# RWKV-7 chunk products moved from half-array tiles to the two diagonal quarters of the array

## The chip, the cores and the metric

One core of a Trainium2 chip runs the whole layer in one launch. The metric is the device time in microseconds, median over runs. Five engines work side by side, each through its own instruction queue in order: TensorE (PE; its weight loads are shown apart as PEld), VectorE (DVE), ScalarE (ACT), GpSimd (POOL) and SyncE (SP, which issues the transfers).

## The reference

A decoder layer on 2048 tokens with model width 1024: an mLSTM group and an RWKV-7 group side by side, then cross-attention into 256 memory tokens, then a SwiGLU block, all in float32. The change touches the RWKV-7 group alone: 8 heads of width 64, each with a 64x64 state that is updated token by token, and a layer norm over each head's 64 outputs:

```python
def rwkv7_scan(r, w, k, v, a, b):
    def step(S, inp):
        r_t, w_t, k_t, v_t, a_t, b_t = inp
        sa = jnp.einsum('bhij,bhj->bhi', S, a_t)
        S = S * w_t[:, :, None, :] + sa[..., None] * b_t[:, :, None, :] + v_t[..., None] * k_t[:, :, None, :]
        return S, jnp.einsum('bhij,bhj->bhi', S, r_t)
...
    y = rwkv7_scan(r, hs(decay), k, v, -kk, kk * a)
    mean = jnp.mean(y, -1, keepdims=True)
    var = jnp.mean(jnp.square(y - mean), -1, keepdims=True)
    y = (y - mean) * lax.rsqrt(var + RWKV_LN_EPS)
```

## The kernel before

The program has a first pass over the input, then the *mixer* (both groups), then the output projection, attention and the SwiGLU block. The mixer makes four passes (`hp` 0 to 3), one per pair of RWKV heads and one mLSTM head. The two RWKV heads of a pair lie in partitions 0 to 63 and 64 to 127. A pass goes over 8 segments of 256 tokens, each cut into 4 chunks of 64 tokens. A *unit* below is one segment of one pass; there are 32.

For each unit, `prepare` projects k, r and v (tiles `kps`, `rps`, `vps`, three half-precision products for each of 8 blocks of the width), computes decays and gates, and builds the chunk matrices: `AR` (decayed a and r), `KB` (decayed k and b), their products with the causal mask (`aps`, line 379), the transposed `KB` (`kbps`, line 391) and the transposed v (line 368). `solve` then inverts the triangular matrices of two units at a time on GpSimd, with small 32x32 products (`pps`, `xps`). `scan` carries the state over the chunks. Its chain for one chunk is: product `ch` column 0 (line 458), copy to `R` on ScalarE (460), product column 1 with `M` (467), copy to `VX` (470), product column 2 (472), and the state update on VectorE (476), which the next chunk's first product waits for. The outputs of four chunks are made at the end of the unit (`yps`, lines 482 and 485), normalised in `tail` and transposed back (`tps`, line 504). `mlstm` does the other group, with its own projections (`qps`, `vops`).

Before, the scan keeps two terms on top of each other in 128 partitions: `VS[:, n, h]` holds the state of head h in that head's 64 partitions and the values v in the other 64, `RR`, `KBt` and `VX` are laid out to match. So one product with 128 rows and 64 columns adds state term and value term in one go. The two heads' products write to the two column halves of the array.

The order of the instructions on each engine is set when the program is built, by a scheduler that follows its own estimates of the times and the dependencies; the code's order is only a start. Buffers come from pools; `pax` has two banks of PSUM for all small results of `prepare`.

Of the kernel before, what the change touches and what calls it, by code (L numbers as in the profile page):

```python
# [105 lines left out]
def rwkv_consts(c, pool, I):  # L106
    nc = c.nc
    par = c.par
    c.mu_s = pool.tile([P, 14], F32, name="mu_s")
    nc.vector.tensor_scalar(c.mu_s, par[:, R_MU:R_MU + 14], DSC, None, op0=ALU.mult)  # L110
    c.mu_c = pool.tile([P, 14], F32, name="mu_c")
    nc.vector.tensor_scalar(c.mu_c, par[:, R_MU:R_MU + 14], -DSC, DSC, op0=ALU.mult, op1=ALU.add)
    c.bones = pool.tile([P, P], F32, name="bones")
    nc.vector.memset(c.bones, 0.0)
    nc.vector.memset(c.bones[0:64, 0:64], 1.0)
    nc.vector.memset(c.bones[64:128, 64:128], 1.0)
    c.ind = pool.tile([P, 2], F32, name="ind")
    nc.vector.memset(c.ind, 0.0)
    nc.vector.memset(c.ind[0:64, 0:1], 1.0)
    nc.vector.memset(c.ind[64:128, 1:2], 1.0)  # L120
# [124 lines left out]
def mixer_pass(c, I, hp, tp, T):  # L245
# [48 lines left out]

    def prepare(sg, u, M):
        g = Ctx()
# [5 lines left out]
        AR = tp.t1.tile([P, 4, P], F32, tag="AR", name="AR")  # L302
        g.RR = next(tp.RR)
        g.M = M
        g.AY = sl.tile([P, 4, 2, 64], F32, tag="AY", name="AY")
        g.KBt = sl.tile([P, 4, 2, 64], F32, tag="KBt", name="KBt")
        g.VS = sl.tile([P, 4, 2, 64], F32, tag="VS", name="VS")
        g.VX = sl.tile([P, 4, 2, 64], F32, tag="VX", name="VX")
        g.bon = sl.tile([P, SGN], F32, tag="bon", name="bon")
        g.W = sl.tile([P, 4, 1], F32, tag="W", name="W")  # L310
        KB = tp.t1.tile([P, 4, 192], F32, tag="KB", name="KB")
# [48 lines left out]
        nc.scalar.copy(KB[:, :, 128:192], KB[:, :, 0:64])  # L360
# [5 lines left out]
        vps = tp.pax.tile([P, 2, P], F32, tag="ax", name="vps")  # L366
        for m in range(2):
            nc.tensor.transpose(vps[:, m], v[:, m * P:(m + 1) * P], c.ident)
        for h in range(2):
            for e in range(2):  # L370
                nc.scalar.copy(g.VS[halves[1 - h], e::2, h], vps[halves[e], :, 64 * h:64 * h + 64])
        for h in range(2):
            nc.gpsimd.tensor_copy(g.VX[halves[1 - h], :, h], g.VS[halves[1 - h], :, h])
        kcs = [slice(64 * (1 - h), 64 * (1 - h) + P) for h in range(2)]
        axs = [tp.pax.tile([P, 4, P], F32, tag="ax", name="aps") for _ in range(2)]
        for n in range(4):
            for h in range(2):
                b = halves[h]
                nc.tensor.matmul(axs[h][:, n], lhsT=KB[b, n, kcs[h]], rhs=AR[b, n], start=True, stop=True)
        for h in range(2):  # L380
            b, ob, aps = halves[h], halves[1 - h], axs[h]
            bc = lambda r, cc: c.mask[r, cc].unsqueeze(1).to_broadcast([r.stop - r.start, 4, 64])
            nc.vector.tensor_tensor(g.M[b], aps[b, :, 0:64], bc(b, b0), ALU.mult)
            nc.vector.tensor_tensor(g.RR[ob, :, h, 0:64], aps[ob, :, 0:64], bc(ob, b0), ALU.mult)
            nc.scalar.copy(g.RR[b, :, h], AR[b])
            nc.vector.tensor_tensor(g.AY[:, :, h], aps[:, :, 64:128], bc(slice(0, P), b1), ALU.mult)
        kps = [tp.pax.tile([P, 4, 64], F32, tag="ax", name="kbps") for _ in range(2)]
        for n in range(4):
            for h in range(2):
                b = halves[h]  # L390
                nc.tensor.transpose(kps[h][:, n], KB[b, n, kcs[h]], c.ident[b, b])
        for h in range(2):
            nc.scalar.copy(g.KBt[:, :, h], kps[h])
        return g

    def solve(MX, NG):
# [3 lines left out]
        MXu = MX.rearrange("p g u t -> p (g u) t")  # L400
# [49 lines left out]
    def scan(sg, g, g2, fresh):  # L450
        y = tp.s2.tile([P, 2, 2, 64], F32, tag="y", name="y")
        if fresh:
            for h in range(2):
                nc.scalar.copy(g.VS[halves[h], 0, h], Sc[halves[h]])
        for n in range(4):
            ch = tp.psc.tile([P, 3, 64], F32, tag="ch", name="ch")
            for h in range(2):
                nc.tensor.matmul(ch[halves[h], 0], lhsT=g.RR[:, n, h, 0:64], rhs=g.VS[:, n, h], start=True, stop=True)
            R = tp.s2.tile([P, 64], F32, tag="R", name="R")
            nc.scalar.copy(R, ch[:, 0])  # L460
            Sw = tp.s2.tile([P, 64], F32, tag="Sw", name="Sw")
            for h in range(2):
                b = halves[h]
                nc.vector.tensor_scalar(Sw[b], g.VS[b, n, h], g.W[b, n], None, op0=ALU.mult)
            for h in range(2):
                b = halves[h]
                nc.tensor.matmul(ch[b, 1], lhsT=g.M[b, n], rhs=R[b], start=True, stop=True)
            for h in range(2):
                b = halves[h]
                nc.scalar.copy(g.VX[b, n, h], ch[b, 1])  # L470
            for h in range(2):
                last = nc.tensor.matmul(ch[halves[h], 2], lhsT=g.KBt[:, n, h], rhs=g.VX[:, n, h], start=True, stop=True)
            for h in range(2):
                b = halves[h]
                dst = g.VS[b, n + 1, h] if n < 3 else g2.VS[b, 0, h] if g2 is not None else Sc[b]
                nc.vector.scalar_tensor_tensor(dst, ch[b, 2], g.W[b, n], Sw[b], op0=ALU.mult, op1=ALU.add)
        yps = tp.psc.tile([P, 2, 2, 64], F32, tag="Y", name="yps")
        with tc.issue_after(last.ins):
            for m in range(2):
                for h in range(2):  # L480
                    for n in (2 * m, 2 * m + 1):
                        nc.tensor.matmul(yps[halves[n % 2], m, h], lhsT=g.RR[:, n, h, 64:128], rhs=g.VS[:, n, h],
                                         start=True, stop=False)
                    for n in (2 * m, 2 * m + 1):
                        nc.tensor.matmul(yps[halves[n % 2], m, h], lhsT=g.AY[:, n, h], rhs=g.VX[:, n, h],
                                         start=False, stop=True)
        nc.vector.tensor_copy(y, yps)

        def tail():
            y4 = y.rearrange("p m h i -> p (m h) i")  # L490
# [5 lines left out]
            nc.scalar.activation(dq, y4, AF.Square)  # L496
# [4 lines left out]
            nc.gpsimd.tensor_tensor(y4, y4, var.unsqueeze(2).to_broadcast([P, 4, 64]), ALU.mult)  # L501
            tps = tp.psx.tile([P, SGN], F32, tag="sx", name="tps")
            for m in range(2):
                nc.tensor.transpose(tps[:, m * P:(m + 1) * P], y[:, m].rearrange("p h i -> p (h i)"), c.ident)
# [127 lines left out]
    for gi, n in enumerate(plan):  # L632
        gs, todo = [], []
        MX = tp.MX.tile([P, n, 4, 64], F32, tag="MX", name="MX")
# [21 lines left out]
def mixer(c, I, T):  # L656
    tc = c.tc
    with ExitStack() as ctx:
        tp = Ctx()
        for name, bufs, space in (("x", 2, None), ("w", 10, None), ("u", 8, None), ("t2", 1, None),  # L660
                                  ("t1", 1, None), ("m2", 2, None), ("k", 2, None), ("sl", 5, None), ("RR", 1, None), ("s2", 2, None), ("MX", 3, None), ("pmm", 2, PSUM),
                                  ("pax", 2, PSUM), ("psc", 1, PSUM), ("psx", 1, PSUM), ("pml", 1, PSUM)):
            kw = {"space": space} if space is not None else {"side": "right"} if name in ("sl", "RR") else {}
            setattr(tp, name, ctx.enter_context(tc.tile_pool(name=f"x{name}", bufs=bufs, reuse_waits="tile", **kw)))

        rr = [tp.RR.tile([P, 4, 2, P], F32, name=f"RR{i}") for i in range(5)]
        for t in rr:
            tc.nc.gpsimd.memset(t[64:128, :, 0, 64:128], 0.0)
            tc.nc.gpsimd.memset(t[0:64, :, 1, 64:128], 0.0)
        tp.RR = cycle(rr)  # L670
# [751 lines left out]
```

## Time and profile before

| what | value |
|---|---|
| median of three runs | 3099.39 us (3096.95 to 3101.4) |
| the profiled execution | 3100.74 us, of which 3099.0 us is the span from the first to the last instruction |
| PE busy, over the span | 2956.4 us, 95% |
| DVE, ACT, POOL busy | 70%, 42%, 39% |
[...]

Busy time of PE is the time in which some matmul is on its way; overlapping matmuls count once. [...] The mixer lies between about 100 and 1235 us.

### The profile page before, as it was taken

To read this page: it belongs to the slowest core of one execution; us is meant where nothing else is said; L and a number is where in the kernel's file an instruction comes from. 1 tells how busy PE (TensorE), PEld (TensorE's weight loads), DVE (VectorE), ACT (ScalarE), POOL (GpSimd) and SP (SyncE) were. 2 spreads that over 40 slices of the span, in tenths; PEclk is the share of its full clock that TensorE was granted. 3 is DMA by queue.
4 is the path that set the end of the run, shared out by engine and by line. 5 is a ranking of instruction groups with operands and counts; after the bars stand their busy time and mean duration, and the time that the engine had idled before them with its cause. 6 is when DMAs were issued, how large, how long until landed. Compare 5 with 4: busy or idle time off the path is not lost. (4 is left out here: it accounts for less than half of the span.)

```text
span 3099.0 us, 55710 instructions
## 1 busy us (share of the span) xinstructions
PE 2956.4 (95%) x20515; PEld 1776.2 (57%) x20515; DVE 2155.9 (70%) x4150; ACT 1299.8 (42%) x3098; POOL 1199.7 (39%) x2189
## 2 busy tenths in 40 slices
PE   7799999999999988999999999999999999899998
PEld 4577777778777767646555554444444444344443
DVE  6568877787687867627788887554454555897975
ACT  6445544554455445506656654222222222423332
POOL 2156654555555665003412134222222221644642
PEclk9899999999999988999999999999999999999999
DMA  8522422232232223555323357122111111554442
GB/s 278 130 76 63 105 70 68 76 97 75 63 80 64 77 70 99 183 167 171 124 76 108 107 194 242 58 67 67 55 55 55 55 58 58 184 185 145 151 144 75
DMA packets 393966, 331.01 MB, mean 107 GB/s; under 512 B 92654, under 2 KB 343772, under 8 KB 392796
## 3 DMA queue, kind: packets, MB, share of 16 engines
q1 hardware_dynamic: 393692, 327.45, 34.5%
q8 instruction: 161, 2.64, 0.3%
q14 instruction: 113, 0.93, 0.1%
HBM read 231.86 MB, written 95.49 MB: 106 GB/s over the span
## 5 line engine op out<-in xcount | busy, mean ns | idle before, releaser
L53 PE MATMUL pp<-u,wb 128*128 128x512 f16 x1232 | 467.5, 379 | 13.5 <-DVE e L1127 10.1
L54 PE MATMUL pp<-u,wb 128*128 128x512 f16 x1232 | 467.7, 380 | 0.0
L55 PE MATMUL pp<-u,wb 128*128 128x512 f16 x1232 | 467.3, 380 | 0.0
L1127 DVE TENSOR_TENSOR e<-pp,e 128x512 f32<-128x512 f32 x308 | 208.5, 689 | 301.6 <-PE pp L55 288.1
L55 PE MATMUL dps<-w,gS 128*128 128x512 f16 x616 | 234.6, 381 | 7.5 <-DVE gS L49 7.5
L54 PE MATMUL dps<-w,gS 128*128 128x512 f16 x616 | 234.7, 381 | 1.7 <-DVE w L49 1.7
L53 PE MATMUL dps<-w,gS 128*128 128x512 f16 x616 | 234.8, 381 | 0.0
L420 POOL TENSOR_TENSOR tmp<-M,X 64x126 f32<-64x126 f32 (+22 forms) x496 | 194.9, 393 | 74.2 <-DMA M<-md 45.9
L422 POOL TENSOR_TENSOR X<-X,tmp 64x126 f32<-64x126 f32 (+22 forms) x496 | 204.3, 412 | 30.1
L54 PEld LDWEIGHTS <-wb 128*128 128x128 f16 x1232 | 120.6, 98 | 157.1 <-issue 13.4
L53 PEld LDWEIGHTS <-wb 128*128 128x128 f16 x1232 | 120.7, 98 | 149.5 <-DMA u<-u_d 3.9
L55 PEld LDWEIGHTS <-wb 128*128 128x128 f16 x1232 | 120.7, 98 | 146.0 <-issue 0.6
L1143 POOL TENSOR_TENSOR S<-raw 128x512 f32<-128x512 f32 x22 | 33.3, 1515 | 411.2 <-DVE wb L49 411.2
L54 PEld LDWEIGHTS <-wh 128*128 128x128 f16 x1280 | 128.0, 100 | 36.0 <-issue 16.1
L53 PE MATMUL qps<-uh,wh 128*128 128x256 f16 x512 | 140.8, 275 | 2.0 <-DVE r L292 1.1
L53 PEld LDWEIGHTS <-wh 128*128 128x128 f16 x1280 | 128.4, 100 | 24.3 <-issue 2.2
L55 PEld LDWEIGHTS <-wl 128*128 128x128 f16 x1280 | 128.3, 100 | 22.5 <-issue 1.9
L53 PE MATMUL vops<-wh,uh 128*128 128x256 f16 x512 | 139.9, 273 | 1.1 <-ACT cv L539 0.8
L55 PE MATMUL qps<-uh,wl 128*128 128x256 f16 x512 | 140.6, 275 | 0.0
L54 PE MATMUL qps<-ul,wh 128*128 128x256 f16 x512 | 140.5, 274 | 0.0
L55 PE MATMUL vops<-wh,ul 128*128 128x256 f16 x512 | 139.8, 273 | 0.0
L54 PE MATMUL vops<-wl,uh 128*128 128x256 f16 x512 | 139.7, 273 | 0.0
(428 smaller groups left out, 7895.2 us busy)
## 6 DMA issues: line engine op xcount, KB each, us to landing
g_d<-e SPq DMA_DIRECT2D x88, 256.0 KB
uh<-u_d SPq DMA_DIRECT2D x144, 128.0 KB
ul<-u_d SPq DMA_DIRECT2D x144, 128.0 KB
h<-h_d SPq DMA_DIRECT2D x32, 512.0 KB
acc<-h_d SPq DMA_DIRECT2D x32, 512.0 KB
u_d<-ub SPq DMA_DIRECT2D x56, 256.0 KB
ga<-g_d SPq DMA_DIRECT2D x32, 384.0 KB
raw<-in_ffn_w_gate_dram SPq DMA_DIRECT2D x22, 512.0 KB
```

The lines of the kernel that those rows point to most:

```text
L53: nc.tensor.matmul(out, lhsT=lhs[0], rhs=rhs[0], start=start, stop=False)
L54: nc.tensor.matmul(out, lhsT=lhs[0], rhs=rhs[1], start=False, stop=False)
L55: nc.tensor.matmul(out, lhsT=lhs[1], rhs=rhs[0], start=False, stop=stop)
L420: nc.gpsimd.tensor_tensor(tv, M[:, s, s + 1:32].unsqueeze(2).to_broadcast(shp), X[:, s, 0:ncl].unsqueeze(1).to_broadcast(shp), ALU.mult)
L422: nc.gpsimd.tensor_tensor(X[:, s + 1:32, 0:ncl], X[:, s + 1:32, 0:ncl], tv, ALU.add)
L1127: add = lambda o, x, y: nc.vector.tensor_tensor(o, x, y, ALU.add)
L1143: nc.gpsimd.tensor_tensor(s[0], a[1][0], a[1][1], ALU.add)
```

## The change

All small RWKV products now work head by head on 64 rows and 64 columns: head 0 on the upper left quarter of the array, head 1 on the lower right. A product with two or three terms is that many products that add up in PSUM (`both`). `VS`, `VX`, `RR` and `AY` are gone: `S`, `V` and `X` hold state, values and solved rows of both heads under each other, `KY` holds the value products, `MX` holds both masked halves. The transposes of v, `KB` and y become ordinary products with an identity (`turn`), that of v with a centring matrix `cent` (identity minus 1/64), which takes the mean out of the values, so that the mean of y need not be computed and subtracted.

```diff
+    c.cent = pool.tile([P, 64], F32, name="cent")
+    for b in (0, 64):
+        nc.vector.tensor_scalar(c.cent[b:b + 64], c.ident[b:b + 64, b:b + 64], -1.0 / 64, None, op0=ALU.add)
...
+    def turn(out, x, by):
+        nc.tensor.matmul(out, lhsT=x, rhs=by, start=True, stop=True)
...
-        nc.scalar.copy(KB[:, :, 128:192], KB[:, :, 0:64])
...
-        vps = tp.pax.tile([P, 2, P], F32, tag="ax", name="vps")
-        for m in range(2):
-            nc.tensor.transpose(vps[:, m], v[:, m * P:(m + 1) * P], c.ident)
-        for h in range(2):
-            for e in range(2):
-                nc.scalar.copy(g.VS[halves[1 - h], e::2, h], vps[halves[e], :, 64 * h:64 * h + 64])
-        for h in range(2):
-            nc.gpsimd.tensor_copy(g.VX[halves[1 - h], :, h], g.VS[halves[1 - h], :, h])
-        kcs = [slice(64 * (1 - h), 64 * (1 - h) + P) for h in range(2)]
-        axs = [tp.pax.tile([P, 4, P], F32, tag="ax", name="aps") for _ in range(2)]
+        vps = tp.pax.tile([P, 4, 64], F32, tag="ax", name="vps")
         for n in range(4):
             for h in range(2):
-                b = halves[h]
-                nc.tensor.matmul(axs[h][:, n], lhsT=KB[b, n, kcs[h]], rhs=AR[b, n], start=True, stop=True)
-        for h in range(2):
-            b, ob, aps = halves[h], halves[1 - h], axs[h]
-            bc = lambda r, cc: c.mask[r, cc].unsqueeze(1).to_broadcast([r.stop - r.start, 4, 64])
-            nc.vector.tensor_tensor(g.M[b], aps[b, :, 0:64], bc(b, b0), ALU.mult)
-            nc.vector.tensor_tensor(g.RR[ob, :, h, 0:64], aps[ob, :, 0:64], bc(ob, b0), ALU.mult)
-            nc.scalar.copy(g.RR[b, :, h], AR[b])
-            nc.vector.tensor_tensor(g.AY[:, :, h], aps[:, :, 64:128], bc(slice(0, P), b1), ALU.mult)
-        kps = [tp.pax.tile([P, 4, 64], F32, tag="ax", name="kbps") for _ in range(2)]
+                turn(vps[halves[h], n], v[halves[h], n * 64:n * 64 + 64], c.cent[halves[h]])
+        nc.scalar.copy(g.V, vps)
+        for o, dst in ((64, g.M), (0, g.KY)):
+            aps = tp.pax.tile([P, 4, P], F32, tag="ax", name="aps")
+            for n in range(4):
+                for h in range(2):
+                    b = halves[h]
+                    nc.tensor.matmul(aps[b, n], lhsT=KB[b, n, o:o + 64], rhs=AR[b, n], start=True, stop=True)
+            nc.vector.tensor_tensor(dst, aps, c.mask.unsqueeze(1).to_broadcast([P, 4, P]), ALU.mult)
+        kps = tp.pax.tile([P, 4, 2, 64], F32, tag="ax", name="kbps")
         for n in range(4):
-            for h in range(2):
-                b = halves[h]
-                nc.tensor.transpose(kps[h][:, n], KB[b, n, kcs[h]], c.ident[b, b])
-        for h in range(2):
-            nc.scalar.copy(g.KBt[:, :, h], kps[h])
+            for e in range(2):
+                for h in range(2):
+                    turn(kps[halves[h], n, e], KB[halves[h], n, 64 * e:64 * e + 64], c.ident[halves[h], halves[h]])
+        nc.scalar.copy(g.KBt, kps)
...
+        def both(out, *parts):
+            for i, (l, r) in enumerate(parts):
+                for b in halves:
+                    last = nc.tensor.matmul(out[b], lhsT=l[b], rhs=r[b], start=i == 0, stop=i == len(parts) - 1)
+            return last
+
         for n in range(4):
             ch = tp.psc.tile([P, 3, 64], F32, tag="ch", name="ch")
-            for h in range(2):
-                nc.tensor.matmul(ch[halves[h], 0], lhsT=g.RR[:, n, h, 0:64], rhs=g.VS[:, n, h], start=True, stop=True)
+            both(ch[:, 0], (g.AR[:, n, 0:64], g.S[:, n]), (g.KY[:, n, 0:64], g.V[:, n]))
...
-            for h in range(2):
-                b = halves[h]
-                nc.vector.tensor_scalar(Sw[b], g.VS[b, n, h], g.W[b, n], None, op0=ALU.mult)
...
+            nc.vector.tensor_scalar(Sw, g.S[:, n], g.W[:, n], None, op0=ALU.mult)
+            both(ch[:, 1], (g.M[:, n, 0:64], R))
+            nc.scalar.copy(g.X[:, n], ch[:, 1])
+            last = both(ch[:, 2], (g.KBt[:, n, 1], g.X[:, n]), (g.KBt[:, n, 0], g.V[:, n]))
+            dst = g.S[:, n + 1] if n < 3 else g2.S[:, 0] if g2 is not None else Sc
+            nc.vector.scalar_tensor_tensor(dst, ch[:, 2], g.W[:, n], Sw, op0=ALU.mult, op1=ALU.add)
...
+            for n in range(4):
+                both(yps[:, n], (g.AR[:, n, 64:128], g.S[:, n]), (g.M[:, n, 64:128], g.X[:, n]), (g.KY[:, n, 64:128], g.V[:, n]))
...
-            mean = tp.s2.tile([P, 4], F32, tag="mean", name="mean")
-            nc.vector.tensor_reduce(mean, y4, AX.X, ALU.add)
-            nc.vector.tensor_scalar(mean, mean, 1.0 / 64, None, op0=ALU.mult)
-            nc.vector.tensor_tensor(y4, y4, mean.unsqueeze(2).to_broadcast([P, 4, 64]), ALU.subtract)
...
-            for m in range(2):
-                nc.tensor.transpose(tps[:, m * P:(m + 1) * P], y[:, m].rearrange("p h i -> p (h i)"), c.ident)
+            for n in range(4):
+                for h in range(2):
+                    turn(tps[halves[h], n * 64:n * 64 + 64], y[halves[h], n], c.ident[halves[h], halves[h]])
```

Since the scheduler builds a new order from the new code, neighbours change on every engine. The first place is TensorE's queue at the end of the first pass, about the last two chunks of its last segment (`sps`, `bps` and `vps` are small products of the next pass's first unit; a row is one product or several that follow each other). Before:

```order
L346 MATMUL sps<-sq,bones 128x256
L467 MATMUL ch<-R,MX 64x64 x2
L364 MATMUL bps<-ta,bones 128x256
L472 MATMUL ch<-VX,KBt 64x64 x2
L368 MATMUL vps<-ident,v 128x128 x2
L458 MATMUL ch<-VS,RR_1573 64x64 x2
L467 MATMUL ch<-R,MX 64x64 x2
L472 MATMUL ch<-VX,KBt 64x64 x2
L482 MATMUL yps<-VS,RR_1573 64x64 x2
```

The same place in the changed program, from the third product of the last chunk but one on:

```order
L450 MATMUL ch<-X,KBt 64x64 x2
L450 MATMUL ch<-V,KBt 64x64 x2
L378 MATMUL aps<-AR,KB 64x128 x15
L450 MATMUL ch<-S,AR 64x64 x2
L450 MATMUL ch<-V,KY 64x64 x2
L378 MATMUL aps<-AR,KB 64x128
L55 LDWEIGHTS wl
L55 MATMUL rps<-uh,wl 128x256
L53 LDWEIGHTS wh
L53 MATMUL rps<-uh,wh 128x256
L54 LDWEIGHTS wh
L54 MATMUL rps<-ul,wh 128x256
```

Before, the three products of the last chunk followed each other with nothing between; now `aps` products stand between its first product and the chunk ahead of it, and (below the rows shown) ten projections and eight `kbps` products ahead of its second product, and eight `kbps`, three `wps` and eleven projections ahead of its third.

The second place is ScalarE's queue near the start of the mixer, where `Em` (mLSTM) needs a transfer of `mb`, and `VS` or `V` is the copy of the transposed v of the first unit. Before:

```order
L784 ACTIVATE b<-b 64x128
L290 ACTIVATE tmu<-vps,mu_s 128x256
L566 ACTIVATE Em<-mb,tk 128x128 x2
L371 COPY VS<-vps 64x2x64 x4
L454 COPY VS<-Sc 64x64 x2
```

Now:

```order
L756 ACTIVATE b<-b 64x128
L372 COPY V<-vps 128x256
L445 COPY S<-Sc 128x64
L544 ACTIVATE Em<-mb,tk 128x128 x2
L290 ACTIVATE tmu<-vps,mu_s 128x256
```

The copies of v and of the state moved ahead of the two `Em`; the second unit's `tmu` moved behind them.

## Rows read from the trace of the kernel before

**Rows 1.** Windows view: length, busy time of each engine (instructions), granted clock, DMA share, GB/s.

```profile
110.00:1235.00 1125.00, 1051.88 (x10507) 835.33 (x10505) 845.04 (x2191) 555.79 (x1686) 612.79 (x1643) 0.95 0.30 76
540.00:560.00 20.00, 20.00 (x186) 16.75 (x185) 13.55 (x37) 8.09 (x28) 5.73 (x15) 1.00 0.42 102
```

**Rows 2.** Windows view of seven stretches; three of them and the sum.

```profile
503.00:521.00 18.00, 13.33 (x98) 9.09 (x97) 13.62 (x32) 7.19 (x22) 13.40 (x37) 0.62 0.03 8
...
1097.00:1142.00 45.00, 33.33 (x347) 24.16 (x346) 29.81 (x76) 18.47 (x57) 19.27 (x56) 0.77 0.23 54
1213.00:1244.00 31.00, 21.53 (x154) 15.17 (x152) 22.23 (x63) 18.34 (x53) 15.95 (x36) 0.67 0.64 192
sum 156.00, PE 118.01 PEld 83.99 DVE 113.57 ACT 73.60 POOL 84.53; mean PE 16.86 PEld 12.00 DVE 16.22 ACT 10.51 POOL 12.08
```

**Rows 3.** Timeline of one chunk's chain: start, length, instructions merged, idle before and releaser.

```profile
503.16 0.34 PE L458 MATMUL ch<-VS,RR 128*64 128x64 f32 x4
...
503.81 0.33 PE L467 MATMUL ch<-R,MX 64*64 64x64 f32 x4 [0.31 <-ACT R L460]
...
504.67 0.34 PE L472 MATMUL ch<-VX,KBt 128*64 128x64 f32 x4 [0.53 <-ACT VX L470]
505.59 0.60 DVE L476 SCALAR_TENSOR_TENSOR VS<-ch,W,Sw 64x64 f32<-64x64 f32 x2
...
506.33 0.34 PE L458 MATMUL ch<-VS,RR 128*64 128x64 f32 x4 [1.33 <-DVE VS L476]
```

**Rows 4.** Timeline of PE: 128-row, 64-column tiles, between two projections.

```profile
627.36 0.27 PE L53 MATMUL vops<-wh,uh 128*128 128x256 f16 x1
627.56 0.34 PE L472 MATMUL ch<-VX,KBt 128*64 128x64 f32 x4
627.73 0.29 PE L482 MATMUL yps<-VS,RR 128*64 128x64 f32 x4
...
628.54 0.29 PE L485 MATMUL yps<-VX,AY 128*64 128x64 f32 x4
628.76 0.28 PE L54 MATMUL vops<-wl,uh 128*128 128x256 f16 x1
```

**Rows 5.** Timeline of PE: 64-row, 128-column tiles (`aps`), and whole-array transposes.

```profile
742.77 1.16 PE L379 MATMUL aps<-AR,KB 64*128 64x128 f32 x8
743.86 0.28 PE L55 MATMUL vops<-wh,ul 128*128 128x256 f16 x1
...
744.09 0.38 PE L504 MATMUL tps<-ident,y 128*128 128x128 f32 x2
744.30 0.27 PE L54 MATMUL vops<-wl,uh 128*128 128x256 f16 x1
```

**Rows 6.** Timeline of PE: the two diagonal quarters (line 467), and `kbps`, among projections.

```profile
604.58 0.27 PE L53 MATMUL qps<-uh,wh 128*128 128x256 f16 x1
604.78 0.33 PE L467 MATMUL ch<-R,MX 64*64 64x64 f32 x4
605.04 0.28 PE L54 MATMUL qps<-ul,wh 128*128 128x256 f16 x1
...
605.58 0.46 PE L391 MATMUL kbps<-ident,KB 64*128 64x64 f32 x4
605.98 0.28 PE L55 MATMUL qps<-uh,wl 128*128 128x256 f16 x1
```

**Rows 7.** Timeline of PE: a long run of 32x32 tiles.

```profile
649.61 0.57 PE L440 MATMUL pps<-T,MX 32*32 32x32 f32 x24
```

**Rows 8.** Waits of PE in the mixer: us in total, times, longest.

```profile
PE aps L379 <- ACT VS L371: 11.4, 5, 7.2
PE vps L53 <- DVE k L292: 10.9, 5, 5.3
```

**Rows 9.** Timeline of ACT near the start of the mixer.

```profile
134.32 0.69 ACT L566 ACTIVATE Em<-mb,tk 128x128 f32<-128x128 f32 x2 [9.14 <-DMA mb<-m_d]
```

**Rows 10.** Costliest groups of DVE in the mixer: one line, busy, mean ns, idle before.

```profile
L464 DVE TENSOR_SCALAR Sw<-VS,W 64x64 f32<-64x64 f32 x230 | 69.4, 302 | 13.4 <-ACT VS L454 8.4
```

More of the change, by code (lines that the diff above doesn't have):

```diff
@@ L301, in prepare @@
         sl = tp.sl
-        AR = tp.t1.tile([P, 4, P], F32, tag="AR", name="AR")
-        g.RR = next(tp.RR)
+        AR = g.AR = sl.tile([P, 4, P], F32, tag="AR", name="AR")
         g.M = M
-        g.AY = sl.tile([P, 4, 2, 64], F32, tag="AY", name="AY")
+        g.KY = sl.tile([P, 4, P], F32, tag="KY", name="KY")
         g.KBt = sl.tile([P, 4, 2, 64], F32, tag="KBt", name="KBt")
-        g.VS = sl.tile([P, 4, 2, 64], F32, tag="VS", name="VS")
-        g.VX = sl.tile([P, 4, 2, 64], F32, tag="VX", name="VX")
+        g.V = sl.tile([P, 4, 64], F32, tag="V", name="V")
+        g.S = sl.tile([P, 4, 64], F32, tag="S", name="S")
+        g.X = sl.tile([P, 4, 64], F32, tag="X", name="X")
         g.bon = sl.tile([P, SGN], F32, tag="bon", name="bon")
         g.W = sl.tile([P, 4, 1], F32, tag="W", name="W")
-        KB = tp.t1.tile([P, 4, 192], F32, tag="KB", name="KB")
+        KB = tp.t1.tile([P, 4, P], F32, tag="KB", name="KB")
         v4 = "p (n t) -> p n t"
@@ L399, in solve @@
         NB = 16 * NG
-        MXu = MX.rearrange("p g u t -> p (g u) t")
+        MXu = MX[:, :, :, 0:64].rearrange("p g u t -> p (g u) t")
         md = c.md.tile([2, 2, NG, 4, 32, 32], F32, tag="md", name="md")
@@ L450, in scan @@
     def scan(sg, g, g2, fresh):
-        y = tp.s2.tile([P, 2, 2, 64], F32, tag="y", name="y")
+        y = tp.s2.tile([P, 4, 64], F32, tag="y", name="y")
         if fresh:
-            for h in range(2):
-                nc.scalar.copy(g.VS[halves[h], 0, h], Sc[halves[h]])
+            nc.scalar.copy(g.S[:, 0], Sc)
+        def both(out, *parts):
[3 more added lines that the diff above has]
+            return last
         for n in range(4):
             ch = tp.psc.tile([P, 3, 64], F32, tag="ch", name="ch")
-            for h in range(2):
-                nc.tensor.matmul(ch[halves[h], 0], lhsT=g.RR[:, n, h, 0:64], rhs=g.VS[:, n, h], start=True, stop=True)
+            both(ch[:, 0], (g.AR[:, n, 0:64], g.S[:, n]), (g.KY[:, n, 0:64], g.V[:, n]))
             R = tp.s2.tile([P, 64], F32, tag="R", name="R")
@@ L461, in scan @@
             Sw = tp.s2.tile([P, 64], F32, tag="Sw", name="Sw")
-            for h in range(2):
-                b = halves[h]
-                nc.vector.tensor_scalar(Sw[b], g.VS[b, n, h], g.W[b, n], None, op0=ALU.mult)
[L465 to L477, printed above, removed]
-        with tc.issue_after(last.ins):
-            for m in range(2):
[L480 to L486, printed above, removed]
+            nc.vector.tensor_scalar(Sw, g.S[:, n], g.W[:, n], None, op0=ALU.mult)
@@ new lines, in scan @@
+            both(ch[:, 1], (g.M[:, n, 0:64], R))
[3 more added lines that the diff above has]
+            nc.vector.scalar_tensor_tensor(dst, ch[:, 2], g.W[:, n], Sw, op0=ALU.mult, op1=ALU.add)
+        yps = tp.psc.tile([P, 4, 64], F32, tag="Y", name="yps")
+        with tc.issue_after(last.ins):
+            for n in range(4):
+                both(yps[:, n], (g.AR[:, n, 64:128], g.S[:, n]), (g.M[:, n, 64:128], g.X[:, n]), (g.KY[:, n, 64:128], g.V[:, n]))
@@ L500, in tail @@
             nc.gpsimd.tensor_tensor(var, var, c.mhalf.to_broadcast([P, 4]), ALU.pow)
-            nc.gpsimd.tensor_tensor(y4, y4, var.unsqueeze(2).to_broadcast([P, 4, 64]), ALU.mult)
+            nc.gpsimd.tensor_tensor(y, y, var.unsqueeze(2).to_broadcast([P, 4, 64]), ALU.mult)
             tps = tp.psx.tile([P, SGN], F32, tag="sx", name="tps")
-            for m in range(2):
-                nc.tensor.transpose(tps[:, m * P:(m + 1) * P], y[:, m].rearrange("p h i -> p (h i)"), c.ident)
+            for n in range(4):
+                for h in range(2):
+                    turn(tps[halves[h], n * 64:n * 64 + 64], y[halves[h], n], c.ident[halves[h], halves[h]])
             yc = tp.s2.tile([P, SGN], F32, tag="dq", name="yc", bufs=1)
@@ L633, in mixer_pass @@
         gs, todo = [], []
-        MX = tp.MX.tile([P, n, 4, 64], F32, tag="MX", name="MX")
+        MX = tp.MX.tile([P, n, 4, P], F32, tag="MX", name="MX")
         for s in range(sg, sg + n):
@@ L660, in mixer @@
         for name, bufs, space in (("x", 2, None), ("w", 10, None), ("u", 8, None), ("t2", 1, None),
-                                  ("t1", 1, None), ("m2", 2, None), ("k", 2, None), ("sl", 5, None), ("RR", 1, None), ("s2", 2, None), ("MX", 3, None), ("pmm", 2, PSUM),
+                                  ("t1", 1, None), ("m2", 2, None), ("k", 2, None), ("sl", 5, None), ("s2", 2, None), ("MX", 3, None), ("pmm", 2, PSUM),
                                   ("pax", 2, PSUM), ("psc", 1, PSUM), ("psx", 1, PSUM), ("pml", 1, PSUM)):
-            kw = {"space": space} if space is not None else {"side": "right"} if name in ("sl", "RR") else {}
+            kw = {"space": space} if space is not None else {"side": "right"} if name == "sl" else {}
             setattr(tp, name, ctx.enter_context(tc.tile_pool(name=f"x{name}", bufs=bufs, reuse_waits="tile", **kw)))
[L666 to L670, printed above, removed]
         for hp in range(4):
```

7 lines of the change are left out of this document (1 added, 6 removed).

## The prediction

> **What bounds the kernel now.** I first cut the span into stages. The change only touches the mixer, so I looked at 110 to 1235 us [rows 1]: PE is busy for 1051.9 of 1125 us, DVE for 845, ACT and POOL for about half. The share of PE says little by itself, because matmuls overlap, so I looked next at a quiet stretch and at the disturbed ones. In the quiet stretch from 540 to 560 us PE is busy for all of 20.00 us at the full clock [rows 1]: there any extra TensorE work adds to the time, and relief on other engines buys nothing. Then I looked for the opposite, where the granted clock of the windows falls. There are seven such stretches behind the start of the mixer, 156 us in all, in which PE is busy for 118 us, so idle for 38 [rows 2]. [...] The lost clock is one minus the share, times the length: 0.38 x 18, 0.23 x 45 and 0.33 x 31 give 27 us for the three that are shown, and all seven give 46.
>
> What happens in them is seen in the timeline [rows 3]: the RWKV chain alone. Its first product starts at 503.16 us, the next chunk's at 506.33, after two ScalarE copies and a state update on VectorE, and in those 3.17 us PE has some 1 us of work. Just behind it the clock falls. So the mixer has two regimes: long stretches where TensorE's own queue is the bound, and short ones where the scheduler found nothing to put between the chain's products, where the chain is the bound and the slow clock comes on top.
>
> **The change, part by part.** *TensorE work per unit.* A float32 product is two instructions in the trace, a transpose one. With 128-row, 64-column tiles the two heads' products run side by side: from the first to the last group of `yps`, 627.73 to 628.54 us, there are seven groups of four instructions, 0.116 us each [rows 4], so 0.058 us for a pair of instructions (a *slot*). 128-column products of 64-row tiles (`aps`) don't overlap: eight instructions take 1.09 us with the way out [rows 5], so 0.136 each, and about 0.116 (two times 0.058) without it. A whole-array transpose takes 0.105 [rows 5], a 64-column transpose of `kbps` about half, 0.06.
>
> Before, a unit has 4 transposes (0.42 us), 16 `aps` instructions (16 x 0.116 = 1.86), 8 `kbps` transposes (0.48), 24 chain products, or 24 slots (1.39), and 16 `yps` products, or 16 slots (0.93): 5.08 us. After, it has 8 products for v (8 slots, 0.46), 16 `aps` of half the columns, two side by side (16 x 0.116 = 1.86), 16 `kbps` products (16 slots, 0.93), 40 chain products (40 slots, 2.32), 24 `yps` products (24 slots, 1.39) and 8 for y (0.46): 7.42 us. The difference is 2.34 us, times 32 units **+75 us**. The reason is plain: half of each array tile used to add state and value term for nothing, and a transpose used to be one instruction.
>
> This rests on the two diagonal quarters running side by side for as long as there is work. The trace of before has them only in groups of four: from 604.78 to 605.04 us [rows 6], with a length (0.33) as that of the column halves (0.34), which are known to overlap. The nearest long run is of 32x32 tiles that also differ in rows and columns: 24 instructions start in 0.4 us [rows 7], 0.016 each; for 32 columns one after the other, half of 0.058 would be wanted. So I take 0.058 per slot for the quarters; the other bound is no overlap at all, as with `aps` of before (rival C).
>
> *Changes of tile shape.* A group of four in the quarters costs 605.04 - 604.58 = 0.46 us between two projections that otherwise follow at 0.11 [rows 6], so 0.35 more, of which 0.12 is work: 0.12 for going in and 0.12 for coming out. Counted over the built order from the first `wps` to the last `tps`, neighbours differ in tile shape 1048 times before and 940 after, because small products of one shape now share a group: 108 x 0.12 = **-13 us**. If changes among small shapes cost half of that, it is -7.
>
> *The stalls.* What the scheduler puts between the chain's products decides them. I counted TensorE work between the 384 chain steps (three per chunk) in both orders, each product at the price above. Before, 34 steps have nothing at all between them and 72 less than 1 us; after, 2 and 8. The ordered rows of the first pass's end are one such place. A step needs about 0.3 to 0.9 us of cover: 503.16 to 503.81 from first to second product and 503.81 to 504.67 from second to third [rows 3], of which the product itself is part. With one `VX` copy and one state update in place of two, the need falls too: the update of 0.60 us [rows 3] becomes one instruction on all 128 partitions, which by the mean of its like (0.302, [rows 10]) is half of that; each is work of 64 elements for every partition.
>
> So the seven stretches mostly go. Their price is 38 us idle and 46 us of lost clock; a slow clock costs nothing while PE is idle, so I count it by the busy share, 118/156: 35 us. Together 73. One stretch of close steps is left near the end in the new order, so I keep 10: **-63 us**. The bounds are 0 (new ones appear elsewhere, since the order comes from estimates) and -73.
>
> *The start.* PE once waits 7.2 us for the copies of v [rows 8], because these stand behind `Em` on ACT, and `Em` waits 9.14 us for its transfer [rows 9]. Now the copies stand ahead of `Em`. But `tmu` of the second unit now stands behind it, with the rest of that unit's v projection's evacuation, and PE can only run ahead by two banks: that is the next thing late. I take **-4**, between 0 and -7.
>
> *VectorE and ScalarE.* `Sw` and the state update halve in number (256 to 128 each, `Sw` alone 128 x 0.302 = 39 us less, [rows 10]), six masked copies per unit become two longer ones, three operations for the mean go, and so do the copies to `RR` and the second `KB` on ScalarE. In the quiet stretches this is hidden under PE. It helps where PE waits for VectorE to empty projections, 10.9 us [rows 8]; I take half, **-5**, between 0 and -11. GpSimd's copies to `VX` go too; nothing waits for GpSimd there that PE waits for, so I count nothing.
>
> The sum is 75 - 13 - 63 - 4 - 5 = -10 us on a span of 3099.0. The profiled run took 3100.74, 1.7 more than its span and 1.4 over the median; from the median of 3099.39 I get **3089 us**. No change that can be told is within 0.2%, 6 us.
>
> [...] In these rows weight loads are hidden: a column-tile slot of 0.058 us has no room for the loads of its two instructions after the matmuls [rows 4]. [...]
>
> **The rivals.** *A: the stalls don't go, or come back elsewhere.* The extra work is sure in the quiet stretches, the gain is not: the scheduler's estimates made the seven stretches, too. Clear of all other terms, half of them left gives 3089 + 32 = 3121 us, all left 3152. For it: the gain rests on an order, not on a removed instruction. Against: 34 steps without cover against 2 is a large difference. The forecast turns into a loss when under 53 of the 73 us go. I give 0.22.
>
> *B: it cancels.* Gain and loss are both some 60 to 75 us, and their difference is small by nature. A third of the stalls left, for instance, gives about 3100. I give 0.19 to anything within 6 us of before.
>
> *C: the quarters don't overlap in long runs.* A slot then costs 0.116: 96 slots of 64 columns and 16 of 128 per unit, 96 x 0.058 + 16 x 0.116 = 7.42 us more, times 32 is 237, so 3326 us. Against it are the groups of four and the 32x32 run. I give 0.04.
>
> *D: all stalls go, and the start and VectorE waits with them.* 75 - 13 - 73 - 7 - 11 = -29, so 3070; with small waits of a us per unit in quiet stretches going as well, near 3060. I give 0.17, and the forecast itself, from about 3075 to 3093, 0.38.
>
> **Range.** From 3064 (most of D) to 3124 (half of A); it leaves out C, the rest of A and the end of D, about 2 in 10. The forecast's own range is 3075 to 3093. Faster is the forecast and D, 0.55; same is B, 0.19; slower is A and C, 0.26.
>
> **What would show it.** Right: PE instructions up, the slots of `yps` and `ch` in the quarters at 0.058 us, PE's busy share in the mixer higher, granted clock near 1.00 in all but one or two places behind the start, the chain's products with projections between them, DVE busy time in the mixer some 100 us lower or more. Wrong: a slot near 0.11 (C); a clock of 0.6 to 0.8 in several stretches, with `R`, `X` or `S` as what PE waits for (A); idle PE in stretches that were quiet before. The likeliest error is in the size of the 63 us, since it weighs an order by its gaps and not by how far ScalarE and VectorE then lag.

## The result and the profile after

The changed kernel takes 3128.22 us (median of four runs, 3122.55 to 3136.95) against 3098.17 for the kernel before beside it: ratio 1.0098, 95% interval 1.0071 to 1.0126. It is slower by about 30 us, where I had forecast 10 us faster; the time lies just beyond my range.

The windows view of the changed kernel's mixer, cut at the same place of the program as [rows 1] (31 us later by then), and of the stretch that was quiet before:

```profile
110.00:1266.00 1156.00, 1080.21 (x14058) 884.63 (x14056) 705.93 (x1759) 453.79 (x1343) 583.83 (x1578) 0.98 0.30 76
540.00:560.00 20.00, 18.21 (x282) 13.85 (x278) 12.31 (x28) 8.36 (x25) 5.21 (x14) 1.00 0.21 42
```

All 31 us arise here; behind the cut both programs need the same time to their ends, 1864 us, with the chains of the last units in both. In the second stretch PE now stands idle for 1.8 of 20 us, which the prediction had named as a sign of being wrong. I split the 31 us in three. Idle time of PE is the length less its busy time: 73.1 before, 75.8 after. The clock's records in these two traces hold two values, a share of 1 and one of 0.5; the granted clock of a stretch is their mean over it, and for the whole span 0.977 before and 0.987 after. Time at the share of 0.5, summed over the records, is 104.4 us before and 42.5 after; half of it is lost, 52 and 21. What is left is TensorE's work at the full clock: 1125.0 - 73.1 - 52.2 = 999.7 before, 1156.6 - 75.8 - 21.3 = 1059.5 after. So **work +60, clock -31, idle +3**. (Where PE is idle at the low clock this counts a little twice, in both.) Over the whole run the same split gives work +65, clock -29, idle -5: the changed kernel makes some 4 us more of its projections ahead of 110 us, where PE stood idle before. VectorE's busy time fell by 139 us, as expected, ScalarE's by 102.

The work is as priced. Timeline of PE in the changed kernel, the two diagonal quarters in a long run:

```profile
602.41 0.33 PE L450 MATMUL ch<-X,KBt 64*64 64x64 f32 x4
602.57 0.28 PE L450 MATMUL ch<-V,KBt 64*64 64x64 f32 x4
602.69 0.28 PE L450 MATMUL yps<-S,AR 64*64 64x64 f32 x4
...
603.97 0.28 PE L450 MATMUL yps<-V,KY 64*64 64x64 f32 x4
604.09 0.28 PE L450 MATMUL ch<-S,AR 64*64 64x64 f32 x4
```

From 602.69 to 604.09 us there are twelve groups of four, 0.117 us each, 0.058 per slot: the same as with the column halves [rows 4].

What changed is for whom PE waits. The waits of PE in the changed kernel's mixer:

```profile
PE tps L296 <- POOL y L478: 23.3, 14, 2.5
PE kbps L296 <- DVE MX L379: 7.7, 1, 7.7
PE ch L450 <- DVE S L464: 7.6, 6, 3.0
PE ch L450 <- ACT R L457: 7.4, 4, 2.9
...
PE ch L450 <- ACT X L461: 2.7, 4, 1.5
```

and those rows of the kernel before that [rows 8] leaves out:

```profile
PE ch L472 <- ACT VX L470: 10.7, 20, 1.1
PE ch L458 <- DVE VS L476: 8.8, 7, 2.3
PE ch L467 <- ACT R L460: 5.4, 14, 1.0
...
PE tps L504 <- POOL y L501: 2.6, 4, 1.2
```

The chain's own waits did fall, the 15 us for `aps` and `vps` that are not the start went (11.4 - 7.2 + 10.9), and 21 us came back at the transposes of y. Why y is late is seen in the timeline of the changed kernel (VectorE, GpSimd and the transposes):

```profile
570.08 0.17 DVE L476 TENSOR_SCALAR var<-var 128x4 f32<-128x4 f32 x1
...
571.43 0.43 POOL L412 TENSOR_TENSOR tmp<-M,X 64x31 f32<-64x31 f32 x1 [7.69 <-DMA M<-md]
571.93 0.47 POOL L414 TENSOR_TENSOR X<-X,tmp 64x31 f32<-64x31 f32 x1
...
574.36 1.01 POOL L477 TENSOR_TENSOR var<-var,mhalf 128x4 f32<-128x4 f32 x1
...
575.74 0.61 POOL L478 TENSOR_TENSOR y<-y,var 128x256 f32<-128x256 f32 x1
...
576.40 0.68 PE L296 MATMUL tps<-ident,y 64*64 64x64 f32 x16 [1.90 <-POOL y L478]
```

The variance is ready at 570.25. The power of it stands behind seven instructions of the solve in GpSimd's queue, the first of which waits for its transfer until 571.43. Over the 28 units that can be followed from variance to transpose, GpSimd begins the power 1.36 us after the variance in the mean (0.37 before). Most begin at once; 11 of the 28 are more than 1 us late, 4 before. And y is ready a median of 0.50 us ahead of its transposes (2.10 before). So the new order calls for y earlier against it, and GpSimd is later in some units.

The start shows the step that I had called "the next thing late":

```profile
131.78 0.69 ACT L544 ACTIVATE Em<-mb,tk 128x128 f32<-128x128 f32 x2 [9.78 <-DMA mb<-m_d]
132.37 0.46 ACT L290 ACTIVATE tmu<-vps,mu_s 128x256 f32<-128x256 f32 x1
132.54 0.41 POOL L545 TENSOR_SCALAR_AFFINE_SELECT Em<-Em 128x256 f32<-128x256 f32 x1 [9.16 <-ACT Em L544]
133.12 0.48 DVE L292 SCALAR_TENSOR_TENSOR v<-vps,mu_c,tmu 128x256 f32<-128x256 f32 x1 [9.07 <-POOL tmu L289]
133.52 0.68 DVE L379 TENSOR_TENSOR MX<-aps,mask 128x512 f32<-128x512 f32 x1
...
134.26 1.97 PE L296 MATMUL kbps<-ident,KB 64*64 64x64 f32 x32 [7.68 <-DVE MX L379]
```

The same transfer of `mb` holds `Em` on ScalarE; GpSimd's `Em` and behind it `tmu` wait for that, VectorE's v of the second unit waits for `tmu` with the masks behind it, and `kbps` waits 7.7 us for these in place of the 7.2 us of `aps`. The copies of v did move ahead, and nothing was gained.

### The profile page after: what moved, and what is told of

Read it like the earlier page. It is cut to its first block, busy times and chain, and to the rows that moved or that the text cites. A ratio compares the mean times of both kernels' runs of the same rounds, so it can differ in the third digit from the quotient of the medians.

```text
span 3130.1 us, 62122 instructions
## 1 busy us (share of the span) xinstructions
PE 2992.5 (96%) x24227; PEld 1834.1 (59%) x24227; DVE 2001.2 (64%) x3669; ACT 1190.4 (38%) x2730; POOL 1162.8 (37%) x2115
```

## The experiments

Theory 1: TensorE's work counts in full, and the idle time came back as waits for GpSimd and for queues. Theory 2: the idle time is set by the scheduler's order and re-forms when one wait is taken away. All ratios are to runs of the kernel before beside it, with 95% intervals; differences from the changed kernel are the ratio less 1.0098, times 3099. *Idle* and *work* are worked out as above, from one profiled execution each. That execution lies up to 6 us from its kernel's median (3123.48 against 3129.70 for `e6_scale_and_copy`), so differences of a few us between two splits say little.

### The price of the work

`e3_no_value`: the second terms of `ch` columns 0 and 2 and the third of `yps` left out.

```diff
-            both(ch[:, 0], (g.AR[:, n, 0:64], g.S[:, n]), (g.KY[:, n, 0:64], g.V[:, n]))
+            both(ch[:, 0], (g.AR[:, n, 0:64], g.S[:, n]))
...
-            last = both(ch[:, 2], (g.KBt[:, n, 1], g.X[:, n]), (g.KBt[:, n, 0], g.V[:, n]))
+            last = both(ch[:, 2], (g.KBt[:, n, 1], g.X[:, n]))
...
-                both(yps[:, n], (g.AR[:, n, 64:128], g.S[:, n]), (g.M[:, n, 64:128], g.X[:, n]), (g.KY[:, n, 64:128], g.V[:, n]))
+                both(yps[:, n], (g.AR[:, n, 64:128], g.S[:, n]), (g.M[:, n, 64:128], g.X[:, n]))
```

> Left out: the value terms (KY or KBt times V) of the chain's first and third product and of the outputs, 24 products per unit, which in the kernel before were the other 64 rows of products that it made anyway. Theory 1 (the extra TensorE work counts in full, at 0.058 us per product): 24 x 0.058 x 32 = 44.5 us less, 3084 (3074 to 3094), PE busy in the mixer some 45 us lower. Theory 2 (the extra products mostly fill time in which TensorE would stand idle or at the lower clock): less than half of that, 3106 to 3128, with more idle time and a lower granted clock in the mixer.

3085.97 us, ratio 0.9943 (0.9928 to 0.9957): 48 us less than the changed kernel. Its mixer:

```profile
110.00:1223.00 1113.00, 1049.74 (x12669) 851.81 (x12668) 698.96 (x1754) 452.53 (x1337) 585.43 (x1578) 0.97 0.31 78
```

Work is 1017.9, 42 less; idle 63. Without the value terms the changed kernel would be the faster one.

`b1_extra_products`, on the kernel before:

```diff
-                    for n in (2 * m, 2 * m + 1):
-                        nc.tensor.matmul(yps[halves[n % 2], m, h], lhsT=g.AY[:, n, h], rhs=g.VX[:, n, h],
-                                         start=False, stop=True)
+                    for q in range(3):
+                        for n in (2 * m, 2 * m + 1):
+                            nc.tensor.matmul(yps[halves[n % 2], m, h], lhsT=g.AY[:, n, h], rhs=g.VX[:, n, h],
+                                             start=False, stop=q == 2)
```

> The kernel before, with its second output product (AY times VX) made three times in place of once: 16 more products per unit in a group that is there anyway, so no new change of tile shape. Changed is the output's value part, which counts three times. Theory 1 (TensorE work in the small tiles counts in full): 16 x 0.058 x 32 = 30 us more than the kernel before, 1.0096 of its time (1.007 to 1.012). Theory 2 (such work fills idle or slow time): under half of that, ratio below 1.005.

3128.78 us, ratio 1.0088 (1.0073 to 1.0103): 27 us more. Theory 1 holds in both directions: neither kernel has slack in which extra products could hide.

### GpSimd and y

`e1_scale_dve` and `e2_no_rstd`, the edit of the second (the first has only its last line):

```diff
-            nc.vector.tensor_scalar(var, var, 1.0 / 64, LN_EPS, op0=ALU.mult, op1=ALU.add)
-            nc.gpsimd.tensor_tensor(var, var, c.mhalf.to_broadcast([P, 4]), ALU.pow)
-            nc.gpsimd.tensor_tensor(y, y, var.unsqueeze(2).to_broadcast([P, 4, 64]), ALU.mult)
+            nc.vector.tensor_scalar(var, var, 0.0, 0.05, op0=ALU.mult, op1=ALU.add)
+            nc.vector.tensor_tensor(y, y, var.unsqueeze(2).to_broadcast([P, 4, 64]), ALU.mult)
```

> The scaling of y by its inverse deviation goes from GpSimd to VectorE; the power itself stays on GpSimd; nothing is left out. Theory 1 (the idle time came back as TensorE waiting for GpSimd's late y): in the changed kernel TensorE waits 23.3 us, 14 times, at the y transposes for this scaling, and about half of the lateness is the wait of the power, half that of the scaling; so the wait falls to about 12 us and the time from 3128 by some 10, to 3112 to 3122. Theory 2 (idle time is set by how the scheduler spreads the work, and any one wait that is taken away re-forms at another place): PE idle in the mixer stays at 70 to 80 us and the time at 3123 to 3133.

3126.47 us, ratio 1.0076 (1.0061 to 1.0091), 7 us less than the changed kernel. On the scale of the two theories (1.0076 times 3098 us) that is 3121.7, just inside the range of theory 1; the idle time is 61 us, under that of theory 2.

> Left out: the inverse deviation of the RWKV layer norm (a constant takes its place), so GpSimd has no part in y; the scaling runs on VectorE. Theory 1: all of the 23.3 us at the y transposes goes, 3128 falls to 3100 to 3110, and PE idle in the mixer from 76 to about 53 us. Theory 2: the idle time re-forms at other waits; 3118 to 3130.

3119.64 us, ratio 1.0051 (1.0033 to 1.0070), 15 us less, on the scale of the theories 3114 and so between them. Its mixer, and waits of PE there:

```profile
110.00:1251.00 1141.00, 1081.93 (x14061) 889.16 (x14061) 714.32 (x1784) 451.65 (x1339) 542.96 (x1518) 0.99 0.30 76
```

```profile
PE ch L450 <- ACT R L457: 10.9, 8, 2.0
PE ch L450 <- ACT X L461: 7.4, 4, 3.3
...
PE ch L450 <- DVE S L464: 4.9, 4, 1.8
PE tps L296 <- DVE y L477: 4.7, 4, 2.0
```

19 us of the wait at the transposes went, and the chain's grew from 17.7 to 23.2. Idle is 59.1, 17 less: of the 23 us that GpSimd's y had cost, part re-formed.

`e4_short_solve` and `b2_short_solve`, one cut in either kernel:

```diff
-        for s in range(31):
+        for s in range(0, 31, 2):
```

> Left out: every second of the 31 substitution steps of the solve on GpSimd, so that GpSimd has some 190 us less to do and y waits less behind it; TensorE's work is unchanged. Theory 1: TensorE's waits for y and for the solve fall from some 30 us to under 10, 3128 falls to 3098 to 3110. Theory 2: the idle time is the chain's own and the order's, 3120 to 3132.

3112.13 us, ratio 1.0030 (1.0019 to 1.0040), 21 us less, idle 60. But not for the reason given: PE's waits in its mixer still begin

```profile
PE tps L296 <- POOL y L478: 14.6, 9, 4.4
PE pps L432 <- DMA T<-t1d: 9.3, 8, 2.4
```

So PE's waits for y and for the solve's products are 24 us, where under 10 were forecast, and GpSimd begins the power 1.38 us after the variance in the mean, as late as with all steps (1.36). A wait for the transfer at the head of the solve, as in the timeline above, would explain why fewer steps behind it don't bring the power forward; this was not tested by itself.

> The kernel before, with every second of the 31 substitution steps of the solve left out, as in the short solve of the changed kernel. Theory 1 (GpSimd's lateness is an ill of the new order, since before TensorE waits only 2.6 us for GpSimd's y): within 6 us of the kernel before, ratio 0.998 to 1.002. Theory 2 (a shorter solve helps any order as much): some 20 us less, as in the changed kernel, ratio 0.993.

3105.83 us, ratio 1.0012 (1.0002 to 1.0022): no gain, idle 72.6. The kernel before hardly waits for GpSimd's y (2.6 us in the rows above), and has nothing to gain.

### ScalarE's queue

`e5_copy_pool`, and `b3_copy_pool` with the same edit of the kernel before:

```diff
-        nc.scalar.copy(M[:, 0:16], X.rearrange("p r c -> p c r"))
+        nc.gpsimd.tensor_copy(M[:, 0:16], X.rearrange("p r c -> p c r"))
```

> The solve's last copy (to M, line 415) goes from ScalarE, where it waits 46.5 us in 14 waits for GpSimd with the chain's copies R and X behind it, to GpSimd itself; nothing is left out. Theory 1 (waits in the queues ahead of the chain's copies are what TensorE waits for at ch and ymps): some 5 to 10 us less than the changed kernel, ratio to before 1.0065 to 1.008. Theory 2 (the idle time re-forms): within 4 us of the changed kernel, or slower by up to 10 since GpSimd, on which y waits, gets 16 more copies; ratio 1.0085 to 1.013.

3118.39 us, ratio 1.0054 (1.0039 to 1.0069), 14 us less than the changed kernel. The wait that was moved, of ScalarE in the changed kernel, then the mixer with the copy on GpSimd, and PE's waits there:

```profile
ACT M L415 <- POOL X L414: 46.5, 14, 6.8
```

```profile
110.00:1251.00 1141.00, 1086.34 (x14059) 891.27 (x14059) 706.39 (x1740) 434.86 (x1310) 600.43 (x1592) 0.98 0.30 75
```

```profile
PE ch L450 <- DVE S L464: 13.9, 12, 3.3
PE tps L296 <- POOL y L478: 10.6, 9, 1.8
...
PE ch L450 <- ACT R L457: 2.4, 2, 2.1
PE ch L450 <- ACT X L461: 2.4, 2, 1.2
```

`ch` waits for R and X 5 us less, for S 6 us more, and y, which this edit doesn't touch, is waited for 13 us less, although GpSimd begins the power as late as before the edit (1.37 us). Idle is 54.7, 21 less. The gain is sure, and larger than either theory had it; its way through the named queue isn't.

> The kernel before with the solve's last copy (line 423) on GpSimd in place of ScalarE, where it waits 23.4 us in 12 waits; nothing is left out. Theory 1 (ScalarE's queue behind that copy is what the chain waits for, and before TensorE waits 16 us for R and VX): 4 to 10 us less, ratio 0.997 to 0.999. Theory 2 (only the new order suffers from it): ratio 0.999 to 1.002.

3099.29 us, ratio 1.0002 (0.9993 to 1.0012): nothing.

`e6_scale_and_copy`, both edits on the changed kernel:

> Both: the scaling of y on VectorE and the solve's last copy on GpSimd, nothing left out. Theory 1: the two gains add up: some 12 to 17 us less than the changed kernel, ratio to before 1.004 to 1.006, PE idle in the mixer 50 to 60 us. Theory 2: idle time stays at 60 us or more, ratio 1.0065 to 1.010.

3129.70 us, ratio 1.0087 (1.0071 to 1.0104). The gains of 7 and 14 us together gave 3, as theory 2 has it, though idle is 58 us and not 60 or more; work is 1065.8, 6 above the changed kernel.

### One part undone

`e7_third_undone`: b's and k's rows of the third product stacked again, the rest left as changed.

```diff
+        nc.scalar.copy(KB[:, :, 128:192], KB[:, :, 0:64])
...
+        for h in range(2):
+            nc.gpsimd.tensor_copy(g.VX[halves[1 - h], :, h], g.V[halves[h]])
...
+                nc.tensor.transpose(kps[h][:, n], KB[b, n, kcs[h]], c.ident[b, b])
...
-            nc.scalar.copy(g.X[:, n], ch[:, 1])
-            last = both(ch[:, 2], (g.KBt[:, n, 1], g.X[:, n]), (g.KBt[:, n, 0], g.V[:, n]))
+            for h in range(2):
+                nc.scalar.copy(g.VX[halves[h], n, h], ch[halves[h], 1])
+            for h in range(2):
+                last = nc.tensor.matmul(ch[halves[h], 2], lhsT=g.KBt[:, n, h], rhs=g.VX[:, n, h], start=True, stop=True)
...
```

(The output products are the same; they read the solved rows out of `VX`.)

> The changed kernel with one part undone: the chain's third product again has b's and k's rows stacked in 128 partitions (VX, KBt and the transposes of KB as before), so a unit has 8 chain products fewer and 8 transposes where it had 16 products; but X takes two copies again, V two on GpSimd, KB one on ScalarE. Nothing is left out. Theory 1 (TensorE's work is what counts): (8 x 0.058 + 16 x 0.058 - 0.48) x 32 = 29 us less than the changed kernel, 3.5 of it given back by the longer chain: ratio to before 1.000 to 1.003. Theory 2 (the copies that the change took away were the gain in idle and slow time): ratio 1.006 to 1.012, with PE idle or slow time in the mixer up by 20 us.

3091.27 us, ratio 0.9967 (0.9954 to 0.9979): 41 us less than the changed kernel and 10 less than the kernel before, the best of all. Its mixer and PE's waits there:

```profile
110.00:1225.00 1115.00, 1065.48 (x12735) 861.44 (x12730) 701.41 (x1748) 489.89 (x1513) 604.06 (x1638) 0.98 0.31 77
```

```profile
PE tps L296 <- POOL y L488: 7.7, 6, 4.5
PE kbps L388 <- DVE MX L382: 7.5, 1, 7.5
PE ch L469 <- ACT VX L467: 7.2, 7, 1.8
PE ch L455 <- DVE S L471: 5.2, 6, 1.8
```

Work is 1038.1, 21 less than with the change whole. 29 were expected, but that left out the changes of tile shape: in the trace neighbours differ in shape 1048 times here and 939 times with the change whole, and at the prediction's 0.12 us this gives 13 back. Idle is 49.5, 26 less, and 6 more are lost to the clock. So the work explains half; the idle time, for which neither theory had foreseen a fall, the other half. y is now ready a median of 1.65 us ahead of its transposes, although GpSimd begins the power nearly as late as with the change whole (1.28 us in the mean). What differs between these two kernels is thus when the order calls for y, not how late GpSimd is.

`e8_third_and_copy` and `e9_third_and_scale` add to it the edit of the copy and that of the scaling:

> The same, with the solve's last copy on GpSimd too, nothing left out. Theory 1: 29 us of TensorE work and the 14 us of the copy add up: ratio to before 0.995 to 0.999, faster than either. Theory 2 (idle time re-forms): 1.000 or above.

3095.32 us, ratio 0.9982 (0.9973 to 0.9991): faster than the kernel before, but 5 us slower than without the edit of the copy, which gives nothing here.

> The kernel with the third product undone, with the scaling of y on VectorE too, nothing left out. There TensorE still waits 7.7 us, 6 times, for GpSimd's y. Theory 1 (that wait is what is left of GpSimd's lateness): up to 6 us less than with the third product undone, ratio to before 0.9945 to 0.9965. Theory 2 (the idle time has reached what the order gives, 50 to 60 us, and re-forms): ratio 0.9965 to 0.999.

3101.82 us, ratio 1.0006 (0.9996 to 1.0016): 12 us worse than without this edit; `ch` then stands idle for 26 us in place of 16.

### Design or order

The swap of `e12_swap` and `e13_third_swap`, and the turn of `e10_value_first` and `e11_third_value_first` (the latter has no second product to turn):

```diff
-        for o, dst in ((64, g.M), (0, g.KY)):
+        for o, dst in ((0, g.KY), (64, g.M)):
```

```diff
-            both(ch[:, 0], (g.AR[:, n, 0:64], g.S[:, n]), (g.KY[:, n, 0:64], g.V[:, n]))
+            both(ch[:, 0], (g.KY[:, n, 0:64], g.V[:, n]), (g.AR[:, n, 0:64], g.S[:, n]))
...
-            last = both(ch[:, 2], (g.KBt[:, n, 1], g.X[:, n]), (g.KBt[:, n, 0], g.V[:, n]))
+            last = both(ch[:, 2], (g.KBt[:, n, 0], g.V[:, n]), (g.KBt[:, n, 1], g.X[:, n]))
```

> The changed kernel with the KY half of the chunk matrices written ahead of the M half: the same instructions, so the time differs only by the order that the scheduler builds. Theory 1 (the order's scatter is small, the idle time is the design's): within 4 us of the changed kernel, ratio to before 1.008 to 1.012. Theory 2 (the scatter is some 10 us, and the changed kernel's order was a bad draw): ratio 1.002 to 1.008, idle 50 to 65 us.

3131.69 us, ratio 1.0095 (1.0077 to 1.0114).

> The kernel with the third product undone, with the same swap: the same instructions as without it. Theory 1: within 4 us of it, ratio to before 0.9955 to 0.998. Theory 2: scatter of 10 us, ratio 0.9965 to 1.001 since that order was a good draw.

3092.65 us, ratio 0.9974 (0.9964 to 0.9984). The same work in another order gives the same time within 3 us, twice, though the idle time moved: 65 in place of 76 (8 of the 11 us lost to a lower clock again), and 56 in place of 50.

> The changed kernel with the value term ahead of the state term in the chain's first and third product, nothing left out and no work added: after a state or an X has arrived, only one pair of products instead of two has to follow. Theory 1 (the chain's length makes the idle time at ch): 0.116 us off each waiting step, and value terms ready to fill the waits: 18.6 us of idle time at ch falls by a third or more, ratio to before 1.005 to 1.008. Theory 2 (the order makes it): anywhere within 15 us of the changed kernel, ratio 1.004 to 1.013, idle 50 to 75 us.

3133.15 us, ratio 1.0102 (1.0086 to 1.0117); idle 80, of it 34 at `ch`, up from 18.6. A shorter step after each state bought nothing.

> The kernel with the third product undone, with the value term first in the chain's first product; nothing left out. Theory 1: 2 to 5 us less than without, ratio to before 0.995 to 0.997. Theory 2: within 10 us of it, ratio 0.9965 to 1.001.

3100.89 us, ratio 1.0002 (0.9992 to 1.0011): 11 us worse than without.

Worked out for all of them:

| kernel | ratio | idle, us | lost clock, us | work, us |
|---|---|---|---|---|
| before; short solve; copy | 1; 1.0012; 1.0002 | 73; 73; 75 | 52; 66; 50 | 1000; 997; 1000 |
| the change; swap; value first | 1.0098; 1.0095; 1.0102 | 76; 65; 80 | 21; 29; 26 | 1060; 1061; 1055 |
| ... scale; copy; both | 1.0076; 1.0054; 1.0087 | 61; 55; 58 | 22; 26; 23 | 1066; 1061; 1066 |
| third undone; swap; copy | 0.9967; 0.9974; 0.9982 | 50; 57; 52 | 27; 25; 26 | 1038; 1037; 1040 |
| ... scale; value first | 1.0006; 1.0002 | 58; 49 | 21; 36 | 1045; 1042 |

The three columns of each kernel add up to its mixer. Work goes with the design, to some 10 us; idle time scatters by 25 us within the whole change and by 9 with the third product undone, and small edits move the whole by up to 14 us. None of the six ways of the whole change comes below 1.005, and none with the third product undone above 1.001. So, as far as these orders show, the loss is the design's, and the size of it, from 17 to 32 us, the order's.

## Why the prediction was wrong

*TensorE work (+75) and tile shapes (-13)*: right as a sum. 62 was forecast and 60 measured in the mixer's profile, 65 over the whole run; taking 24 products per unit out gave back 48 us for 44.5. The changes of shape fell as counted, from 1047 to 939 in the traces; the price of one was not tested by itself.

*Quarters side by side*: right; rival C is out: the long run of quarters above has 0.058 us per slot. The weight loads in that run of quarters have 0.135 us each in the trace and start while earlier products are still on their way: PEld and PE are both busy for all 1.40 us from 602.69 to 604.09.

*The stalls (-63)*: this step failed, in one of its halves. With 10 of 73 kept, the forecast was 30 us of clock and 33 of idle time. The clock gave 31, but since the idle time that was to go with it stayed, part of this agreement may be luck. The idle time was to fall, and the chain's waits did shrink, but over the mixer it went from 73 to 76 us. The runs show in its place that idle time isn't owned by the chain: 23 us stood at the transposes of y, and with GpSimd taken out of y's way altogether 17 us of idle time came off. That does not prove y to be the one cause, since moving the solve's copy, which leaves y alone, took off 21. My count weighed the cover between the chain's steps only and put GpSimd at nothing; it never looked at how far ahead y stands of its transposes, which went from 2.10 to 0.50 us, although y's way over GpSimd was in the trace. What happened is rival A, stalls that come back elsewhere; with half of them left it gave 3121.

*The start (-4)*: nothing came. I named what would be late next, `tmu` behind `Em`, and then didn't believe its price: 7.7 us for 7.2.

*VectorE (-5)*: PE's wait of 10.9 us for VectorE at `vps` is gone and VectorE is busy for 139 us less, but idle time as a whole shows no gain, so the term is part of the same failure.

For the mixer's idle time the forecast was thus 73 less 33, 4 and 5, so 31 us; measured were 76. These 45 us, less 3 for work and clock that came out better, are the 42 by which the mixer missed (+32 in place of -10).

What stays open: why idle time is 55 to 80 us with the whole change and 49 to 58 with the third product undone, by which way the copy on GpSimd gained 14 us with the whole change and nothing in the two other kernels, and why the clock came back while the idle time did not. The power on another engine, with its result kept, was not run.

## What to carry to other kernels

Where TensorE is busy for nearly all of a stage, as for 1051.9 of 1125 us here, price its added work first and count it as sure: here 60 us arrived where 62 were forecast. Count waits that a new order is to remove as a chance, not as a sum: here the idle time came back (73 us before, 76 after) wherever something else was late, and the candidates are read from what each engine's queue holds ahead of the results that TensorE wants next. Then undo a change part by part: here the part with most added work and least relief cost 41 us, and the rest of the change was a gain of 10.

## What the runs showed of the hardware

With nearly the same idle time in the mixer, 76 and 73 us, TensorE stood at half its clock for 42.5 us in the changed order and for 104.4 before, so idle time alone doesn't tell the lost clock. How the idle time is parted doesn't tell it either: 65 of 76 us lie in gaps over 1 us in the changed kernel and 39 of 73 before, but `b2_short_solve` has 42 of 73 there and 133 us at half the clock, and `e13_third_swap` 35 of 56 and 48 us. Nor do the transposes of `KB`, which became products: with the third product undone they are back, and the five kernels of that kind stand at half the clock for some 42 to 72 us, twice the lost clock of the table above. And a power of 128 x 4 elements takes GpSimd 1.01 us in the timeline above, more than the scaling of 128 x 256 (0.61), so its short operand doesn't make it a cheap link in a chain.
